# Convolution pairs and decay matrices handed out between attention units, and a different set of buffers at the start

## The chip, the cores and the metric

The kernel runs on one core of a Trainium2 chip. The metric is the time of one execution on the device in microseconds. The engines are named as in the profile: PE (matrix products, with PEld for its weight loads), DVE (vector), ACT (activations), POOL (GpSimd), and SP, whose queue issues nearly all DMA transfers.

## The reference

Four transformer layers on one sequence of 256 tokens of width 1024, all in float32: two layers of a first block (latent attention beside a gated linear recurrence, then a feed-forward part), then two layers of a second block. The change is in the mixing of the second block and in the first microseconds of the kernel. The second block's mixing, cut to what matters:

```python
proj = h @ w_in                                   # h = rmsnorm(x)
q, k, v, z, xbc, dt = split(proj)
attn = dilated_attention(rotary(q), rotary(k), v) # 8 heads of 64, softmax under a mask
xbc = silu(causal_depthwise_conv(xbc, conv_w, conv_b))      # 1536 channels, 4 taps
xs, bm, cm = split(xbc)                           # 1024, 256, 256 channels
dt = softplus(dt + dt_bias)
a_cs = cumsum(dt * -exp(a_log))                   # per head, in chunks of 128 tokens
m_mat = (cm . bm) * exp(where(t >= s, a_cs[t] - a_cs[s], -inf))
y = m_mat @ (xs * dt) + carry_over_of_chunk_0 + d_skip * xs
y = grouped_rmsnorm(y * silu(z))
x = x + concat(attn, y) @ w_out
x = x + swiglu(rmsnorm(x))
```

The first layer of the first block begins with `h = rmsnorm(x)` and the projections of `h` to the latents `c_q` (384 columns) and `c_kv` with `k_pe` (288 columns).

## The kernel before

Activations are kept transposed (128 channels on the partitions, 256 tokens along the row). Each weight is streamed from device memory in tiles of up to 128x1024 by `Stream.load`: a DMA into one of three buffers `wf`, a copy rounded to fp32r on ACT (`wh`, line 399), and the remainder by a subtraction on DVE (`wl`, line 400; on POOL for the weight units named in `WL_POOL`). There are six buffers each of `wh` and `wl`. A product of full precision is then three passes on PE (lines 428 to 430: high by high, high by low, low by high), in the two-pass form of lines 449 and 450 in the feed-forward parts.

A scheduler orders the instructions of each engine. It follows the order of the program text where it can and moves instructions forward when, by its own estimate, their inputs and buffers are ready. So the text's order, the number of buffers and the estimates together decide what stands behind what; at run time each engine works through its own list in order.

`layer_b` computes the second block's mixing. Behind the projections come the softplus of `dt` (lines 1038 to 1048, a chain of small DVE instructions), its product with `-exp(a_log)` (`aa`, line 1053), the cumulative sum as a product on PE (lines 1055 and 1056) and, from it, eight decay matrices: `acs` is transposed (line 1068), written to device memory (`ad`, line 1073), read back spread over all partitions (tile `r`, line 1079), and POOL subtracts the column's own value (line 1080) and adds a causal mask (line 1081); ACT takes the exponential (line 1082). Then `attention` runs six units (one group of heads each). A unit is: scores on PE (line 578), mask and maximum on DVE (lines 582, 584), exponentials on ACT (line 588), the division on DVE (line 590), transposes on PE (line 602), a copy on ACT (line 604), and the product with the values on PE (line 613). In the text the six convolution pairs stand behind the attention: a pair is a weight unit of 48 products on PE, the scaling by the norm on DVE (line 1127), one tap on ACT (line 1132) and three on DVE (line 1134) for each of two channel groups, and a gate by tanh (lines 1137 and 1138). The scheduler already lifts these pairs in between the attention units. Behind them come the products of the decay matrices (line 1174) with the chunk products, `d_skip` (line 1154, on POOL), the gate by `z`, the norm and the output projection.

At the start, `norm_prep` splits `x` in two parts (lines 473 and 474) and calls `norm_scale`, which squares and adds mostly on POOL (lines 502 to 506). `WARM` products on a matrix of ones (line 424) stand ahead of the first real products.

## Time and profile before

| | us |
|---|---|
| median of 3 runs | 1481.76 |
| lowest, highest | 1475.6, 1490.52 |
| the profiled execution's own time | 1484.13 |
| span of the profile (first to last instruction) | 1482.3 |
| PE busy | 1441.9 |
| DVE busy | 1146.6 |
| ACT busy | 822.2 |
| POOL busy | 302.5 |

The profiled execution took 1484.13, of which 1482.3 lie between its first and last instruction. All times in the rows below are microseconds from the start of that span. The second block's mixing lies at about 780 to 925 (its layer 0) and 1125 to 1270 (its layer 1). PEclk is the clock granted to PE as a share of its full speed; 0.5 is the lower of its two levels, 1.2 instead of 2.4 GHz.

### The profile page before, as it was taken

How to read it: one execution, taken by the hardware profiler on the slowest of the kernel's cores; microseconds unless marked ns; L12 is line 12 of the kernel's file. 1: busy time of each engine (PE TensorE's matmuls, PEld its weight loads, DVE VectorE, ACT ScalarE, POOL GpSimd, SP SyncE). 2: the span in 40 equal slices, each digit the busy share in tenths (PEclk: the TensorE clock that was granted, in tenths of full speed). 3: DMA queues.
4: the chain of work that ended last, by engine and by line, in shares of the span. 5: the costliest groups of instructions: out<-in, count | busy, mean ns of one | idle time of the engine just before them, and what ended most of it. 6: DMA issues, size and time to landing. Idle time of an engine off the chain costs nothing.

```text
span 1482.3 us, 26346 instructions
## 1 busy us (share of the span) xinstructions
PE 1441.9 (97%) x10176; PEld 1305.3 (88%) x10176; DVE 1146.6 (77%) x1747; ACT 822.2 (55%) x1415; POOL 302.5 (20%) x302
## 2 busy tenths in 40 slices
PE   8999999999999999999999899999999889999998
PEld 7989998888998999888888799888888789988887
DVE  6796788876677867987666999887766799988754
ACT  6665447655474644666445464476545465466643
POOL 3600020000143101100013724500002634510001
PEclk9999999999999999999999899999999789999999
DMA  6633546555654255655555444555556533556553
GB/s 202 216 128 116 174 162 205 193 165 179 195 186 156 92 160 167 199 194 187 157 185 193 123 152 147 165 190 187 155 188 203 154 115 115 171 188 197 167 178 110
DMA packets 85949, 248.77 MB, mean 168 GB/s; under 512 B 8960, under 2 KB 28224, under 8 KB 85824
## 3 DMA queue, kind: packets, MB, share of 16 engines
q1 hardware_dynamic: 85536, 246.56, 52.4%
q8 instruction: 80, 1.31, 0.4%
q10 hardware_dynamic: 288, 0.52, 0.1%
q14 instruction: 45, 0.37, 0.1%
HBM read 245.94 MB, written 1.11 MB: 167 GB/s over the span
## 4 chain that ended last, share of the span: by engine, by line
PE 76%; DVE 11%; DMA 6%; ACT 2%; issue 2%; POOL 1%; SPq 0%; DVEq 0%; POOLq 0%; ACTq 0%
PE mm L449 25%; PE mm L450 13%; PE mm L429 7%; PE mm L430 7%; PE mm L428 7%; PE at L449 7%; DVE wl L400 4%; PE at L450 4%; DMA wf<-in_wa 3%; DMA wf<-in_wb 2%; DVE t L1134 2%; ACT wh L399 2%; PE at L578 1%; DVE xs L474 1%; PE rc L872 1%
## 5 line engine op out<-in xcount | busy, mean ns | idle before, releaser
L400 DVE TENSOR_TENSOR wl<-wf,wh 128x1024 fp32r<-128x1024 f32 (+2 forms) x500 | 578.8, 1167 | 178.9 <-ACT wh L399 175.9
L399 ACT ACTIVATE wh<-wf 128x1024 fp32r<-128x1024 f32 (+3 forms) x508 | 491.4, 970 | 341.9 <-PE mm L429 90.6
L449 PE MATMUL mm<-xs,wh 128*128 128x512 f32 x960 | 337.1, 394 | 1.7 <-DVE xs L474 1.6
L450 PE MATMUL mm<-xs,wl 128*128 128x256 f32 x960 | 268.7, 281 | 0.0
L449 PEld LDWEIGHTS mm<-xs,wh 128*128 128x128 f32 x960 | 179.7, 187 | 42.7 <-DVE xs L474 1.4
L428 PE MATMUL mm<-xs,wh 128*128 128x256 f32 x704 | 208.2, 296 | 0.3 <-ACT q L750 0.3
L430 PE MATMUL mm<-xs,wl 128*128 128x256 f32 x704 | 206.6, 293 | 0.7 <-DVE wl L400 0.7
L429 PE MATMUL mm<-xs,wh 128*128 128x256 f32 x704 | 207.2, 294 | 0.0
L502 POOL TENSOR_TENSOR m<-x 128x512 f32<-128x512 f32 x27 | 35.7, 1322 | 769.8 <-DVE x L655 616.9
L450 PEld LDWEIGHTS mm<-xs,wl 128*128 128x128 f32 x960 | 181.7, 189 | 0.5
L449 PE MATMUL at<-xs,wh 128*128 128x512 f32 x448 | 157.8, 394 | 0.1
L430 PEld LDWEIGHTS mm<-xs,wl 128*128 128x128 f32 x704 | 139.5, 198 | 3.8 <-issue 2.6
L428 PEld LDWEIGHTS mm<-xs,wh 128*128 128x128 f32 x704 | 139.4, 198 | 3.9 <-issue 2.5
L429 PEld LDWEIGHTS mm<-xs,wh 128*128 128x128 f32 x704 | 139.6, 198 | 2.7 <-issue 2.3
L450 PE MATMUL at<-xs,wl 128*128 128x256 f32 x448 | 126.1, 281 | 0.0
L429 PE MATMUL mm<-r,wh 128*128 128x256 f32 x384 | 109.2, 285 | 0.0
L430 PE MATMUL mm<-r,wl 128*128 128x256 f32 x384 | 108.6, 284 | 0.0
L428 PE MATMUL mm<-r,wh 128*128 128x256 f32 x384 | 107.9, 284 | 0.5 <-DVE x L559 0.5
L449 PEld LDWEIGHTS at<-xs,wh 128*128 128x128 f32 x448 | 83.9, 187 | 19.3 <-PE mm L450 0.4
L449 PE MATMUL mm<-t,wh 128*128 128x512 f32 x256 | 90.7, 395 | 0.0
L449 PE MATMUL mm<-h,wh 128*128 128x512 f32 x256 | 90.7, 395 | 0.0
L450 PEld LDWEIGHTS at<-xs,wl 128*128 128x128 f32 x448 | 84.8, 189 | 0.1
(331 smaller groups left out, 2817.7 us busy)
## 6 DMA issues: line engine op xcount, KB each, us to landing
wf<-in_fa SPq DMA_DIRECT2D x120, 512.0 KB, 3.9
wf<-in_fb SPq DMA_DIRECT2D x120, 512.0 KB, 4.1
wf<-in_wa SPq DMA_DIRECT2D x100, 512.0 KB, 4.3
wf<-in_wb SPq DMA_DIRECT2D x72, 512.0 KB, 3.7
wf<-in_fa SPq DMA_DIRECT2D x32, 192.0 KB, 2.4
...
```

Of the source, the lines that this page charges most:

```text
L399: S.activation(wh[:, :c], f, AF.Copy)
L400: (G if self.i in self.pool else V).tensor_tensor(out=wl[:, :c], in0=f, in1=wh[:, :c].bitcast(F32), op=ALU.subtract)
L428: PE.matmul(ps, lhsT=sh, rhs=mh, start=start, stop=False)
L429: PE.matmul(ps, lhsT=sh, rhs=ml, start=False, stop=False)
L430: PE.matmul(ps, lhsT=sl, rhs=mh, start=False, stop=stop)
L449: PE.matmul(wide, lhsT=wh[:, j, c0:c0 + P], rhs=xs[k], start=k == 0, stop=False)
L450: PE.matmul(wide[:, 1], lhsT=wl[:, j, c0:c0 + P], rhs=xs[k][:, 0], start=False, stop=k == tot - 1)
L474: V.scalar_tensor_tensor(out=dstl, in0=src, scalar=scale, in1=dsth.bitcast(F32), op0=ALU.mult, op1=ALU.subtract)
L502: G.tensor_tensor(out=z, in0=x[:, c:c + 2], in1=x[:, c:c + 2], op=ALU.mult)
L578: PE.matmul(ps[:, h], lhsT=q, rhs=k[:, 0:n * P], start=True, stop=True)
L872: PE.matmul(ps[o:o + ms, g], lhsT=zb[:, 0:ms], rhs=zb.rearrange("p (n a h) -> p n a h", a=2, h=h)[:, :, 1], start=True, stop=True, tile_po ...
L1134: V.scalar_tensor_tensor(out=cv[:, m], in0=xp[:, m, j:j + T], scalar=w(j), in1=cv[:, m], op0=ALU.mult, op1=ALU.add)
```

## The change

Four things are changed together.

In `layer_b` the convolution pairs become a function `conv_pair`, and so does the making of a decay matrix. The first pair is computed ahead of the softplus; `attention` calls `between(u)` in each of its six units, which gives out one more pair (units 0 to 4), the loads of all eight matrices (unit 0) and one matrix's arithmetic (units 1 to 5); the remaining three follow behind.

The matrix's arithmetic is now ACT's: for each of four heads a Relu of `acs - row` (with scale -1 and the column's value as bias), then one exponential with scale -1. The causal mask is not added any more; instead two of the three chunk products (`cb`) are multiplied by the triangle `triu` on DVE, where ACT only copied them. `d_skip` leaves POOL: it is folded into the addition of the chunk's result, one DVE instruction for each of two channel groups instead of one for both. `WL_POOL` is empty, so that all weight remainders are DVE's.

In the first layer the latent projections are given out ahead of the norm's scale, whose squares are now made on ACT and added on DVE.

The first four weight tiles are loaded into the four buffers `h` (not in use that early) instead of `wf`, and `WARM` goes from 9 to 14.

```diff
     WFB, WSB = 3, 6
-    WARM = 9
-    WL_POOL = (7, 9)
+    WARM = 14
+    EARLY = 4
+    WL_POOL = ()
...
             self.pool = WL_POOL if name.startswith("wb") else ()
+            self.early = EARLY if name == "wa0" else 0
...
-                wf = wp.tile([P, 1024], F32, tag="wf", name=nm("wf"), bufs=WFB)
+                if self.early:
+                    self.early -= 1
+                    wf = sb("h", [P, 1024])
+                else:
+                    wf = wp.tile([P, 1024], F32, tag="wf", name=nm("wf"), bufs=WFB)
...
-    def norm_scale(eps):
-
+    def norm_scale(eps, pool=True):
+
+        if not pool:
+            acc = sb("m", [P, 2, T])
+            sq = sb("m", [P, 2, T])
+            for c in (0, 2, 4, 6):
+                z = sq if c else acc
+                S.activation(z, x[:, c:c + 2], AF.Square)
+                if c:
+                    V.tensor_tensor(out=acc, in0=acc, in1=sq, op=ALU.add)
+            a = acc[:, 0]
+            V.tensor_tensor(out=a, in0=a, in1=acc[:, 1], op=ALU.add)
+            return rsqrt(token_sums(a), 2, 1.0 / D, eps)
...
-    def norm_prep(gname, eps):
+    def norm_prep(gname, eps, between=None):
+
         xs = cp.tile([P, NC, 2, T], F32R, tag="xs", name=nm("xs"))
-        xh, xl = xs[:, :, 0], xs[:, :, 1]
         for c in range(NC):
-            split(xh[:, c], xl[:, c], x[:, c], fm(gname, c))
-        r = norm_scale(eps)
-        rb = bcast_rows(r, "rc")
-        return [xh[:, c] for c in range(NC)], [xl[:, c] for c in range(NC)], [xs[:, c] for c in range(NC)], r, rb
+            split(xs[:, c, 0], xs[:, c, 1], x[:, c], fm(gname, c))
+        xh, xl = [xs[:, c, 0] for c in range(NC)], [xs[:, c, 1] for c in range(NC)]
+        if between:
+            between(xh, xl)
+        r = norm_scale(eps, between is None)
+        return xh, xl, [xs[:, c] for c in range(NC)], r, bcast_rows(r, "rc")
...
+                if between:
+                    between(u)
                 pt = psq(next(tags)).rearrange("p (h k) -> p h k", k=P)
...
+        def latents(xh, xl):
+            for n in (384, 288):
+                lat.append([psm(), psm()])
+                lin_tm([p[:, :n] for p in lat[-1]], st.next() + st.next(), xh, xl, n)
+
+        xh, xl, _, r, rb = norm_prep(f"nmix_a{l}", EPS1, latents if l == 0 else None)
         if l == 1:
+            latents(xh, xl)
...
+        conv = {}
+        pairs = [4, 5, 0, 1, 2, 3]
+        c4 = []
+
+        def conv_pair():
+            i = len(conv)
+            p = pairs[i]
+            if i % 2 == 0:
+                c4.append(sb("t", [P, 2, 2, T]))
+            ps = psm().rearrange("p (m t) -> p m t", m=2)
+            u = st.next()
+            for m in range(2):
+                lin_fm(ps[:, m], u, m * P, xh, xl)
+            xp = sb("Z", [P, 2, T + 4])
+            G.memset(xp[:, :, 0:3], 0.0)
+            V.tensor_tensor(out=xp[:, :, 3:T + 3], in0=ps, in1=rows(rb, 2), op=ALU.mult)
+            cv = c4[-1][:, i % 2]
+            for m in range(2):
+                c = 2 * p + m
+                w = lambda j: wh2[:, 4 * c + j:4 * c + j + 1]
+                S.activation(cv[:, m], xp[:, m, 0:T], AF.Identity, scale=w(0), bias=wh2[:, 48 + c:49 + c])
+                for j in range(1, 4):
+                    V.scalar_tensor_tensor(out=cv[:, m], in0=xp[:, m, j:j + T], scalar=w(j), in1=cv[:, m],
+                                           op0=ALU.mult, op1=ALU.add)
+            tz = sb("m", [P, 2, T])
+            S.activation(tz, cv, AF.Tanh)
+            V.scalar_tensor_tensor(out=cv, in0=tz, scalar=1.0, in1=cv, op0=ALU.add, op1=ALU.mult)
+            conv[p] = cv
+
+        conv_pair()
...
-        pT = psq("rc")
-        PE.transpose(pT[0:32, 0:P], acs.rearrange("p t h -> p (t h)"), ident)
-        arow = sb("hv", [32, 2, P])
-        S.activation(arow[:, 0], pT[0:32, 0:P], AF.Copy)
-        S.activation(arow[:, 1], pT[0:32, 0:P], AF.Exp)
-        ad = dp.tile([32, 2, P], F32, tag="ad", name=nm("ad"), bufs=1)
-        nc.sync.dma_start(out=ad, in_=arow)
+
         decay = {}
-        neg4 = neg.rearrange("p (o t) -> p o t", o=1).to_broadcast([P, 4, P])
-        for g, t, q4 in itertools.product(range(2), repeat=3):
-            h0 = 8 * g + 4 * q4
-            E = sb("r", [P, 4, P])
-            nc.sync.dma_start(out=E, in_=ad[16 * t + h0:16 * t + h0 + 4, 0].partition_broadcast(P))
-            G.tensor_tensor(out=E, in0=E, in1=bc(acs[:, t], h0, 4, P), op=ALU.subtract)
-            G.tensor_tensor(out=E, in0=E, in1=neg4, op=ALU.add)
-            S.activation(E, E, AF.Exp)
-            decay[g, t, q4] = E
+        loaded = []
+
+        def decay_rows():
+            pT = psq("rc")
+            PE.transpose(pT[0:32, 0:P], acs.rearrange("p t h -> p (t h)"), ident)
+            arow = sb("hv", [32, 2, P])
+            S.activation(arow[:, 0], pT[0:32, 0:P], AF.Copy)
+            S.activation(arow[:, 1], pT[0:32, 0:P], AF.Exp)
+            ad = dp.tile([32, 2, P], F32, tag="ad", name=nm("ad"), bufs=1)
+            nc.sync.dma_start(out=ad, in_=arow)
+            for g, t, q4 in itertools.product(range(2), repeat=3):
+                h0 = 8 * g + 4 * q4
+                E = sb("r", [P, 4, P])
+                nc.sync.dma_start(out=E, in_=ad[16 * t + h0:16 * t + h0 + 4, 0].partition_broadcast(P))
+                decay[g, t, q4] = E
+                loaded.append((E, t, h0))
+            for j in range(2):
+                nc.sync.dma_start(out=into[64 * j:64 * j + 64], in_=ad[16 + j:32:2, 1].partition_broadcast(64))
+
+        def decay_exp():
+            E, t, h0 = loaded.pop(0)
+            for h in range(4):
+                S.activation(E[:, h], E[:, h], AF.Relu, scale=-1.0, bias=acs[:, t, h0 + h:h0 + h + 1])
+            S.activation(E, E, AF.Exp, scale=-1.0)
+
         into = sb("h", [P, 8, P])
-        for j in range(2):
-            nc.sync.dma_start(out=into[64 * j:64 * j + 64], in_=ad[16 + j:32:2, 1].partition_broadcast(64))
-
-
-        qT = sb("t", [P, 4, T])
-        kT = sb("OF", [P, T])
-        ps = psq("at")
-        for t in range(2):
-            PE.transpose(ps[:, t * P:t * P + P], ak[t], ident)
-        S.activation(kT, ps[:, 0:T], AF.Copy)
-        for t in range(2):
-            ps = psq("at").rearrange("p (c k) -> p c k", c=4)
-            for c in range(4):
-                PE.transpose(ps[:, c], aq[t][:, c * P:c * P + P], ident)
-            S.activation(qT[:, :, t * P:t * P + P], ps, AF.Copy, scale=0.125)
+
+        def between(u):
+            if u == 0:
+                decay_rows()
+            else:
+                decay_exp()
+            if u < 5:
+                conv_pair()
...
-        mh, ml = attention(groups, qk, lambda a, i: av[a][:, i % 2], (dil0, dil1), *oT, ("at", "rc"), AH_B)
+        mh, ml = attention(groups, qk, lambda a, i: av[a][:, i % 2], (dil0, dil1), *oT, ("at", "rc"), AH_B, between)
+
+        while loaded:
+            decay_exp()
...
-        for p in range(4):
-            o = fmc[f"dsk{l}"][0] + 2 * p
-            G.tensor_tensor(out=conv[p], in0=conv[p], in1=bc(pfm, o, 2, T), op=ALU.mult)
...
-            S.activation(cb.rearrange("p g t -> p (g t)"), ps[:, 0:T], AF.Copy)
+            if i < 2:
+                V.tensor_tensor(out=cb, in0=ps[:, 0:T].rearrange("p (g t) -> p g t", g=2),
+                                in1=triu.rearrange("p (o t) -> p o t", o=1).to_broadcast([P, 2, P]), op=ALU.mult)
+            else:
+                S.activation(cb.rearrange("p g t -> p (g t)"), ps[:, 0:T], AF.Copy)
...
-            V.tensor_tensor(out=conv[p], in0=conv[p], in1=py, op=ALU.add)
+            for m in range(2):
+                V.scalar_tensor_tensor(out=conv[p][:, m], in0=conv[p][:, m], scalar=fm(f"dsk{l}", 2 * p + m), in1=py[:, m],
+                                       op0=ALU.mult, op1=ALU.add)
```

In the order of the instructions this shows at three places. The first is POOL in layer 0's second block, from the last step of the queries' rotation on (`r` are the decay matrices, `Z` the convolution's input). Before:

```order
L1014 TENSOR_TENSOR q_9019<-q_9019,rt_1528_9027 128x8x16
L400 TENSOR_TENSOR wl_9524<-wf_9522,wh_9523 128x1024
L400 TENSOR_TENSOR wl_9530<-wf_9528,wh_9529 128x1024
L1126 MEMSET Z_9507 128x2x3
L1080 TENSOR_TENSOR r_9072<-r_9072,acs_9060 128x512
L1080 TENSOR_TENSOR r_9077<-r_9077,acs_9060 128x512
L1081 TENSOR_TENSOR r_9072<-r_9072,msk 128x512
L1080 TENSOR_TENSOR r_9082<-r_9082,acs_9060 128x512
L1081 TENSOR_TENSOR r_9077<-r_9077,msk 128x512
```

Now:

```order
L1039 TENSOR_TENSOR q_9022<-q_9022,rt_1528_9030 128x8x16
L1078 MEMSET Z_9385 128x2x3
L1078 MEMSET Z_9497 128x2x3
L1078 MEMSET Z_9597 128x2x3
L1078 MEMSET Z_9707 128x2x3
```

Twenty large instructions (four remainders, eight subtractions, eight masks) are gone from this place, and only small fills are left until the state products.

The second is ACT at the first attention units of the same layer (`hv` is the transposed cumulative sum, `pr` the probabilities, `Z` and `t` the convolution's input and result, `PT` the transposed probabilities). Before:

```order
L1071 ACTIVATE hv_9067<-rc_9065 32x128
L588 ACTIVATE pr_9143,den_9144<-at_9135,mx_9141 128x128 x4
L588 ACTIVATE pr_9159,den_9160<-rc_9151,mx_9157 128x128 x4
L1137 ACTIVATE m_9367<-t_9294 128x512
L399 ACTIVATE wh_9599<-wf_9598 128x1024
L399 ACTIVATE wh_9605<-wf_9604 128x1024
L1132 ACTIVATE t_9294<-Z_9431,wh_1596_9292 128x256 x2
L604 ACTIVATE PT_9172<-at_9167 128x512
```

Now, from the second softmax to the first transposed probabilities:

```order
L606 ACTIVATE pr_9191,den_9192<-rc_9183,mx_9189 128x128 x4
L1163 ACTIVATE r_9206<-r_9206,acs_9159 128x128 x4
L1163 ACTIVATE r_9208<-r_9208,acs_9159 128x128 x4
L1163 ACTIVATE r_9210<-r_9210,acs_9159 128x128 x4
L404 ACTIVATE wh_9648<-wf_9647 128x1024
L1163 ACTIVATE r_9212<-r_9212,acs_9159 128x128 x4
L1164 ACTIVATE r_9206<-r_9206 128x512
L404 ACTIVATE wh_9654<-wf_9653 128x1024
L1163 ACTIVATE r_9214<-r_9214,acs_9159 128x128 x2
L1164 ACTIVATE r_9208<-r_9208 128x512
L1084 ACTIVATE t_9323<-Z_9385,wh_1529_9035 128x256 x2
L1163 ACTIVATE r_9214<-r_9214,acs_9159 128x128
```

The Relus of four matrices and part of a fifth, which need loads to have landed, now stand on ACT between the second softmax and the copy of the first transposed probabilities.

The third is ACT in the opening (`xs` is the split input, `m` the squares, `wh` a weight's high part). Before:

```order
L473 ACTIVATE xs_154<-x,pfm 128x256 x2
L399 ACTIVATE wh_90<-wf_89 128x768
L473 ACTIVATE xs_154<-x,pfm 128x256 x2
L399 ACTIVATE wh_97<-wf_96 128x768
L473 ACTIVATE xs_154<-x,pfm 128x256 x2
```

Now:

```order
L478 ACTIVATE xs_159<-x,pfm 128x256 x2
L508 ACTIVATE m_276<-x 128x512
L404 ACTIVATE wh_90<-h_89 128x768
L478 ACTIVATE xs_159<-x,pfm 128x256 x2
L508 ACTIVATE m_277<-x 128x512
L404 ACTIVATE wh_97<-h_96 128x768
L478 ACTIVATE xs_159<-x,pfm 128x256 x2
```

A square of 128x512 now stands ahead of each of the first three weight copies, and the copies read from `h`.

## Rows read from the trace of the kernel before

**Rows 1.** The page's first part: PE's busy time, share of the span, instructions.

```profile
PE 1441.9 (97%) x10176; PEld 1305.3 (88%) x10176; DVE 1146.6 (77%) x1747; ACT 822.2 (55%) x1415; POOL 302.5 (20%) x302
```

**Rows 2.** Waits of PE: who waited for whom, us in total, times, longest.

```profile
PE rc L602 <- DVE pr L590: 12.8, 4, 5.4
PE rc L1055 <- DVE aa L1053: 5.2, 2, 3.0
```

**Rows 3.** Busy time in stretches: PE, PEld, DVE, ACT, POOL; PEclk, DMA share, GB/s.

```profile
804.60:820.00 15.40, 13.11 (x61) 11.62 (x61) 9.02 (x17) 6.84 (x26) 5.73 (x5) 0.67 0.54 156
832.70:847.00 14.30, 8.90 (x42) 7.13 (x42) 14.30 (x13) 4.25 (x11) 13.96 (x10) 0.64 0.17 55
...
855.00:860.00 5.00, 5.00 (x42) 4.31 (x42) 5.00 (x10) 3.53 (x6) 0.00 (x0) 1.00 0.71 240
...
1151.50:1168.00 16.50, 13.52 (x58) 12.22 (x58) 8.84 (x18) 6.67 (x26) 4.83 (x3) 0.59 0.43 136
1181.70:1192.00 10.30, 7.27 (x31) 6.08 (x31) 10.30 (x10) 2.81 (x7) 10.30 (x9) 0.67 0.18 57
1196.40:1205.00 8.60, 4.59 (x20) 3.61 (x20) 8.60 (x17) 6.29 (x14) 0.38 (x2) 0.80 0.16 61
```

**Rows 4.** DVE's timeline: start, length, instruction, count, idle before.

```profile
804.72 2.27 DVE L1048 SCALAR_TENSOR_TENSOR dtt<-dtt,pol 128x32 f32<-128x32 f32 x1
...
830.23 2.70 DVE L1134 SCALAR_TENSOR_TENSOR t<-Z,wh,t 128x256 f32<-128x256 f32 x2
...
849.27 0.47 DVE L1134 SCALAR_TENSOR_TENSOR t<-Z,wh,t 128x256 f32<-128x256 f32 x1
...
851.05 0.68 DVE L590 TENSOR_TENSOR pr<-pr,den 128x512 f32<-128x512 f32 x1
...
1154.05 0.19 DVE L1048 SCALAR_TENSOR_TENSOR dtt<-dtt,pol 128x32 f32<-128x32 f32 x1
```

**Rows 5.** DVE's groups from 800 to 925: busy us, mean ns, idle before.

```profile
L400 DVE TENSOR_TENSOR wl<-wf,wh 128x1024 fp32r<-128x1024 f32 x24 | 32.0, 1336 | 1.1 <-ACT wh L399 1.1
L1134 DVE SCALAR_TENSOR_TENSOR t<-Z,wh,t 128x256 f32<-128x256 f32 x36 | 25.4, 738 | 0.3 <-ACT t L1132 0.3
L590 DVE TENSOR_TENSOR pr<-pr,den 128x512 f32<-128x512 f32 x6 | 7.7, 1277 | 0.0
L1138 DVE SCALAR_TENSOR_TENSOR t<-m,t 128x512 f32<-128x512 f32 x6 | 6.7, 1110 | 0.9 <-ACT m L1137 0.8
```

**Rows 6.** POOL's groups over the whole span, both layers: busy us, mean ns, idle before.

```profile
L1081 POOL TENSOR_TENSOR r<-r,msk 128x512 f32<-128x512 f32 x16 | 24.0, 1510 | 0.0
L1080 POOL TENSOR_TENSOR r<-r,acs 128x512 f32<-128x512 f32 x16 | 22.5, 1424 | 3.8 <-DMA r<-ad 3.8
L400 POOL TENSOR_TENSOR wl<-wf,wh 128x1024 fp32r<-128x1024 f32 x8 | 19.9, 2492 | 7.8 <-ACT wh L399 7.8
```

**Rows 7.** ACT's timeline at the first softmax of layer 0's second block.

```profile
813.16 0.37 ACT L588 ACTIVATE pr<-at,mx 128x128 f32<-128x128 f32 x1
813.42 0.19 ACT L588 ACTIVATION_READ_ACCUMULATOR pr<-at,mx 128x1 f32 x1
```

**Rows 8.** The 16 loads of line 1079 (`r<-ad`): us from issue to landing.

```profile
DMA to landing us min/median/max: 4.3/5.9/8.2
```

**Rows 9.** The opening: timelines of PE and ACT.

```profile
10.15 0.69 PE L429 MATMUL mm<-wl,xs 128*128 128x384 f32 x1 [2.14 <-DVE wl L400]
...
13.20 0.52 PE L430 MATMUL mm<-wh,xs 128*128 128x384 f32 x1
...
15.53 0.34 PE L430 MATMUL mm<-wh,xs 128*128 128x384 f32 x1
...
29.90 0.39 PE L430 MATMUL mm<-xs,wl 128*128 128x256 f32 x1 [0.74 <-DVE wl L400]
...
13.24 0.85 ACT L399 ACTIVATE wh<-wf 128x768 fp32r<-128x768 f32 x1 [1.96 <-DMA wf<-in_wa]
...
27.53 1.06 ACT L399 ACTIVATE wh<-wf 128x1024 fp32r<-128x1024 f32 x1 [2.87 <-DMA wf<-in_wa]
```

60 lines of the change are left out of this document (22 added, 38 removed).

## The prediction

> **What bounds the kernel now.** First the busy shares [rows 1]: PE is busy 1441.9 of 1482.3 us, 97%. PE sets the time, and whatever the change does can only come out of the 40 us in which PE is idle and out of products that run at the lower clock. So next I looked for where these lie: the stretches with their granted clock, and PE's list of waits. In the second block's mixing PE waits for DVE at two kinds of place [rows 2]: 12.8 us in four waits for the divided probabilities (line 590) ahead of the transposes, and 5.2 us in two waits for `aa`, the end of the softplus chain, ahead of the cumulative sum.
>
> Five stretches hold these waits [rows 3]. Idle time is length less PE's busy time: 2.3 and 5.4 us in layer 0; 3.0, 3.0 and 4.0 in layer 1: 17.7 together. In each of the five the clock also falls to its lower level once PE has waited; length times (1 - PEclk) is 15.4 x 0.33 = 5.1, 14.3 x 0.36 = 5.1, 16.5 x 0.41 = 6.8, 10.3 x 0.33 = 3.4, 8.6 x 0.20 = 1.7, together 22.1. Some half clock falls into the idle time itself; I take off 1.5 as an estimate. What PE loses there is then about 17 us in layer 0 and 21 in layer 1, 38 in all. That is the purse of the main part of the change.
>
> Why is DVE late? It is itself full there (14.30 of 14.30, 10.30 of 10.30 [rows 3]), but many of its instructions take far longer than they need to. Two conv taps take 2.70 us at 830, while one takes 0.47 at 849 [rows 4]. The last softplus step, a 128x32 instruction, takes 2.27 us at 804.7 and 0.19 in the other layer [rows 4]. POOL is busy 13.96 of 14.30 us in the slow stretch and not at all at 855 to 860 [rows 3]: DVE's instructions stretch when POOL runs large ones.
>
> **The change part by part.** *POOL's work leaves.* Per layer, eight subtractions of 1.42, eight masks of 1.51 and four remainders of 2.49 us go [rows 6], besides four `d_skip` products. What this frees on DVE I sum from layer 0's groups [rows 5], each against its undisturbed length [rows 4]: taps 25.4 - 36 x 0.47 = 8.5; divisions 7.7 - 6 x 0.68 = 3.6; gates, of the same shape, 6.7 - 6 x 0.68 = 2.6; the softplus step 2.27 - 0.19 = 2.1. That is 16.8 us per layer.
>
> *DVE's added work.* Four remainders come over: 4 x 1.34 = 5.3 at the disturbed mean [rows 5], an upper bound. Two triangle products of 128x256 at no more than 0.47 each, and `d_skip` as eight half-width instructions instead of four full ones, 8 x 0.47 - 4 x 0.68: another 2. DVE's balance is 16.8 - 7.3 = 9.5 us less work per layer. It can also take back time in which it waits for PE at half clock: it is idle 6.4 us in the first stretch of layer 0 and 7.7 in that of layer 1 [rows 3]. So on DVE's path the gain is 9.5 at least and 16 to 17 at most per layer; on PE's path it is 17 and 21.
>
> *The cumulative sum.* In the order DVE's chain up to `aa` is unchanged, four remainders among it; without POOL's remainder beside it, its last step ends 2.1 us sooner in layer 0, where PE waits 2.2. Most of that wait goes, and with it the reason for the half clock behind it.
>
> *ACT's added work.* 32 Relus of 128x128 per layer. No row shows a Relu with a bias; the nearest is the softmax's exponential of the same size and bias, 0.37 long, with the next instruction starting 0.26 after it [rows 7]. Bounds are 8.3 and 11.8 us per layer; I take 0.30 each, 9.6, since neighbours overlap. The exponentials stay. ACT is busy 4.25 of 14.30 us in the slow stretch [rows 3], so the sum fits; what matters is order. The Relus of four matrices and more stand ahead of the first `PT` copy. Following the lists from the second softmax: four times 1.2 us of Relus, two weight copies of 1.06 [rows 9], two exponentials, the fifth matrix's first three Relus, two taps and a tanh, about 11 us, until that copy. PE in this time has the products of one and a half pairs and a full pair, some 100 at 0.12 us (42 in 5.00 [rows 3]), 12 us, before it needs `PT`. That leaves a margin of one or two microseconds: ACT's new work is hidden, barely.
>
> The Trainium skill, "ScalarE: Activation LUTs", section "What ACT_TABLE_LOAD costs", gives an activation with a bias pointer as some 280 ns and 0.833 ns per element, of which about 93 ns overlap with the next one. By that a Relu would be an estimated 0.29 us and the 32 of a layer 9.4, in place of 9.6; no run here shows it yet.
>
> *The loads of the matrices.* They are issued from SP at the same place as before, behind one more weight load. Landing takes 4.3 to 8.2 us [rows 8]; POOL used to stand waiting for the first, now ACT does, with weight copies, taps and `PT` queued behind it, and PE behind those. The order puts two softmaxes and three more instructions between the store and the first Relu, so I cost this at nothing; if the landing takes its maximum instead of its median 5.9, the margin above is gone and PE waits about 2 us.
>
> *What is late next.* With the taps short, I expect PE to wait for about 1 us at the cumulative sum, 1 at the later transposes, 1 to 2 for a remainder that now queues on DVE, and 2 at the output projection, whose inputs still pass over POOL (the gate by `z`) and DVE. That is 5 to 6 us per layer, in waits shorter than those of [rows 3], all of over 2 us, behind which the clock fell. So of 17 I count 12 in layer 0, of 21 I count 15 in layer 1; both lie between DVE's bounds.
>
> *The opening.* PE starts its second kind of product at 10.15 after a wait of 2.14 for the first remainder, runs at half clock (a product 0.52 long at 13.2, 0.34 at 15.5), and later the first weight behind the constants keeps ACT waiting 2.87 until 27.53 and PE until 29.90 [rows 9]. With POOL's squares gone the first remainder should come about 1.5 us sooner, although ACT now makes a square ahead of it (about 0.55, half of the copy of 1024 columns at 27.53 [rows 9]); the longer warm-up leaves no gap. With four loads in buffers of their own, the wait of 1.96 for the fourth at 13.24 goes too [rows 9]. What ends the stage is the load that ACT waits for at 27.53; its buffer comes free behind these copies, so by an estimate of 1.5 to 3.5 us earlier, and the load with it. Gain 3; bounds 0 (the load comes no earlier) and 4.5 (all of it counts). Behind 30 us PE is full, so it is kept.
>
> The sum is 12 + 15 + 3 = 30 us off the profiled execution's 1484.1, which is 1454. That execution lies 2.4 above the median of 1481.8, so against the median I forecast **1452**.
>
> **The rivals.** *Everything recovered*: PE never waits for long; 38 + 4.5 - 2 = 40.5 us, 1441. For it: DVE's bound of 16 to 17 nearly reaches layer 0's 17. Against it: DVE stays full.
>
> *One fall of the clock per layer stays*, because one of the late waits passes 2 us. Price: the first stretch of layer 0 shows it, 5.1 of clock; two layers, 10 us: 1462. The Trainium skill, "TensorE: Matmul & The Clock Gate", section "HAM oscillation — how this bites in real kernels", describes waits each of which makes the stretch behind it start at the lower clock again; this trace agrees in all five stretches [rows 3].
>
> *ACT becomes the late engine* (slower): the first Relu waits for its load in ACT's list, taps and `PT` come late, and through the two `Z` buffers and four PSUM banks every pair stalls PE. This decides the sign if PE then loses more per layer than now, over 19 us, which is about three waits of 2.3 with their 5 us of clock each, 22 per layer: 44 against 38, less the opening's 3: 1485. For it: the thin margin. Against it: ACT was idle for 10 of 14.3 us, and a load that lands in 6.
>
> *The change does not do what it says*: the scheduler had lifted the pairs already, so handing them out may be no change, and the time would come from POOL's relief alone. That gives DVE's lower bound, 9.5 per layer, and an opening of 0: 1463.
>
> **How the numbers follow.** Chances: forecast 0.50 (1445 to 1459), everything recovered 0.12 (1438 to 1445), one fall or POOL's relief alone together 0.27 (1459 to 1471), ACT late 0.11 (1471 to 1500). The range of 1440 to 1470 leaves out most of the last case and little else. One per cent is 14.8 us, about the spread of the three runs shown and about what a measurement of this kernel can tell from no change. Faster than 1467: 0.50 + 0.12 + most of 0.27, 0.82. Slower than 1496.6: a third of the last case, 0.04. The rest, 0.14, is no change.
>
> **What would show it.** In the profile after: no waits of PE of over 2 us for line 608 (the division) or for `aa`; PEclk at full in both mixings; taps at 0.4 to 0.5 each; POOL nearly idle until the state products; ACT busier by 9 to 10 us per layer; the first remainder at about 8.5 and pair products from about 26. Wrong would be: a wait of ACT for `r<-ad` over 2 us, PE waiting for ACT's `PT` or for remainders, or stretches of half clock without a wait ahead of them.

## The result, and the profile after

The changed kernel takes 1457.05 us (median of four, 1454.24 to 1460.24) against 1481.55 for the kernel before: a ratio of 0.9836, 95% interval 0.9802 to 0.9871. That is 24.5 us or 1.6% faster. The forecast was 1452, with a range of 1440 to 1470. The profiled execution took 1456.76 us, 27.4 less than that of before.

The first part of the page after (busy time, share of the span, instructions) answers to [rows 1]:

```profile
PE 1425.7 (98%) x10186; PEld 1290.3 (89%) x10186; DVE 1117.2 (77%) x1769; ACT 839.2 (58%) x1477; POOL 221.6 (15%) x248
```

PE is idle for 29 us in place of 40. Its waits after (who waited for whom, us in total, times, longest) answer to [rows 2]. Line 608 is the division, which was line 590; 1131 is the cumulative sum, which was 1055:

```profile
PE mm L433 <- DVE m L575: 3.6, 2, 2.3
PE rc L1131 <- DVE aa L1129: 3.1, 2, 1.8
PE mm L433 <- ACT wh L404: 2.8, 2, 1.7
...
PE mm L435 <- DVE wl L405: 2.3, 3, 0.8
PE rc L622 <- DVE pr L608: 1.5, 2, 0.8
```

The waits for the divided probabilities have gone from 12.8 us to 1.5, those for `aa` from 5.2 to 3.1. What is last now is `m` at the output projection (line 575). Six stretches of both mixings, read as [rows 3] (length, busy time of PE, PEld, DVE, ACT, POOL, then PEclk):

```profile
800.00:804.00 4.00, 2.25 (x20) 2.04 (x20) 3.86 (x10) 2.33 (x5) 2.00 (x3) 1.00 0.41 123
...
842.00:847.00 5.00, 3.47 (x28) 3.09 (x27) 4.93 (x10) 5.00 (x12) 0.11 (x1) 1.00 0.39 120
1133.00:1138.00 5.00, 3.61 (x31) 3.40 (x31) 4.76 (x13) 2.66 (x5) 2.99 (x5) 1.00 0.54 143
...
1176.00:1181.00 5.00, 3.46 (x27) 3.09 (x27) 4.93 (x10) 5.00 (x12) 0.00 (x0) 1.00 0.36 113
900.00:908.00 8.00, 5.34 (x43) 5.03 (x41) 6.56 (x13) 4.20 (x5) 4.11 (x5) 1.00 0.50 164
908.00:914.00 6.00, 6.00 (x37) 5.95 (x38) 4.94 (x7) 1.45 (x2) 5.15 (x7) 0.72 0.39 128
```

In each of the first four PE still loses 1.4 to 1.8 us, but the granted clock stays at its upper level (PEclk 1.00). Only behind the output projection of layer 0, where PE is idle for 2.7 us, does the clock fall once: 6.0 x 0.28 = 1.7 us. Of the five falls of [rows 3] none is left in its place.

DVE's groups in layer 0, 796 to 910, answer to [rows 5] (busy us, mean ns, idle before):

```profile
L405 DVE TENSOR_TENSOR wl<-wf,wh 128x1024 fp32r<-128x1024 f32 x29 | 36.5, 1259 | 4.8 <-ACT wh L404 4.7
L1086 DVE SCALAR_TENSOR_TENSOR t<-Z,wh,t 128x256 f32<-128x256 f32 x36 | 15.5, 477 | 0.0
L608 DVE TENSOR_TENSOR pr<-pr,den 128x512 f32<-128x512 f32 x6 | 4.1, 688 | 0.1
L1090 DVE SCALAR_TENSOR_TENSOR t<-m,t 128x512 f32<-128x512 f32 x6 | 4.1, 688 | 0.7 <-ACT m L1089 0.7
```

Taps went from 738 ns to 477, divisions from 1277 to 688, gates from 1110 to 688. ACT's group of Relus in the same stretch:

```profile
L1163 ACT ACTIVATE r<-r,acs 128x128 f32<-128x128 f32 x32 | 10.2, 395 | 2.0 <-DMA r<-ad 2.0
```

They overlap, and 10.2 us is the time in which at least one of them runs. What one costs shows where several stand in a row:

```profile
832.82 2.16 ACT L1163 ACTIVATE r<-r,acs 128x128 f32<-128x128 f32 x7
```

Less the length of the last, 2.16 - 0.40 us hold six of them, 0.29 from one start to the next, so 32 take 9.4 us. ACT waits 2.0 us for the first matrix. PE and ACT in the opening (start, length, idle before) answer to [rows 9]:

```profile
8.02 0.44 PE L434 MATMUL mm<-wl,xs 128*128 128x384 f32 x1 [0.37 <-DVE wl L405]
...
25.88 0.39 PE L433 MATMUL mm<-xs,wh 128*128 128x256 f32 x1 [1.68 <-ACT wh L404]
...
24.77 1.06 ACT L404 ACTIVATE wh<-wf 128x1024 fp32r<-128x1024 f32 x1 [3.31 <-DMA wf<-in_wa]
```

To see where the time went I cut the run into stages, by DVE's last addition to the residual in each: line 675 ends a feed-forward, line 577 a second-block mixing. In the kernel after these additions start at:

```profile
778.32 0.41 DVE L675 TENSOR_TENSOR x<-x,mm 128x256 f32<-128x256 f32 x1
...
927.42 0.41 DVE L577 TENSOR_TENSOR x<-x,m 128x256 f32<-128x256 f32 x1
...
1112.74 0.41 DVE L675 TENSOR_TENSOR x<-x,mm 128x256 f32<-128x256 f32 x1
...
1260.79 0.41 DVE L577 TENSOR_TENSOR x<-x,m 128x256 f32<-128x256 f32 x1
...
1445.04 0.88 DVE L675 TENSOR_TENSOR x<-x,mm 128x256 f32<-128x256 f32 x2 [4.53 <-PE mm L455]
```

In the kernel before (lines 655 and 559) the same five start at:

```profile
781.79 0.41 DVE L655 TENSOR_TENSOR x<-x,mm 128x256 f32<-128x256 f32 x1
...
945.66 0.41 DVE L559 TENSOR_TENSOR x<-x,m 128x256 f32<-128x256 f32 x1
...
1128.82 0.41 DVE L655 TENSOR_TENSOR x<-x,mm 128x256 f32<-128x256 f32 x1
...
1291.89 0.41 DVE L559 TENSOR_TENSOR x<-x,m 128x256 f32<-128x256 f32 x1
...
1472.73 0.87 DVE L655 TENSOR_TENSOR x<-x,mm 128x256 f32<-128x256 f32 x2 [4.39 <-PE mm L450]
```

So up to the first of these mixings 3.5 us are won, in the mixings 163.9 - 149.1 = 14.8 and 163.1 - 148.0 = 15.1, and in the two feed-forwards behind them, which nobody touched, 2.2 and 3.4 us are lost. The last two figures were in no step of the prediction. The cut is good to about 1 us: in layer 0 DVE's last addition starts 5.8 us behind PE's first product of the feed-forward in the kernel before and 4.6 in the kernel after. Cut by the first and last products of the feed-forwards on PE, the mixings win 13.6 and 15.5 and the feed-forwards lose 1.0 and 3.9.

### The profile page after: what moved, and what is told of

The parts are those of the page before. It is cut to its first block, busy times and chain, and to the rows that moved or that the text cites. A ratio compares the mean times of both kernels' runs of the same rounds, so it can differ in the third digit from the quotient of the medians.

```text
span 1455.0 us, 26376 instructions
## 1 busy us (share of the span) xinstructions
PE 1425.7 (98%) x10186; PEld 1290.3 (89%) x10186; DVE 1117.2 (77%) x1769; ACT 839.2 (58%) x1477; POOL 221.6 (15%) x248
## 4 chain that ended last, share of the span: by engine, by line
PE 87%; DVE 6%; ACT 2%; DMA 2%; issue 2%; POOL 1%; SPq 0%; POOLq 0%; DVEq 0%; ACTq 0%
PE mm L454 25%; PE mm L455 13%; PE mm L434 11%; PE mm L435 11%; PE mm L433 11%; PE at L454 7%; PE at L455 4%; DVE wl L405 2%; DVE xs L479 1%; PE at L596 1%; DMA wf<-in_wb 1%; ACT wh L404 1%; PE at L633 1%; PE rc L897 1%; PE at L622 1%
## 5 line engine op out<-in xcount | busy, mean ns | idle before, releaser
L405 DVE TENSOR_TENSOR wl<-wf,wh 128x1024 fp32r<-128x1024 f32 (+3 forms) x504 | 577.2, 1155 | 182.0 <-ACT wh L404 179.9
L454 PEld LDWEIGHTS mm<-xs,wh 128*128 128x128 f32 x960 | 179.7, 187 | 43.9 <-DVE xs L479 2.9
L433 PE MATMUL mm<-xs,wh 128*128 128x256 f32 x704 | 203.2, 289 | 1.7 <-ACT wh L404 1.7
L434 PE MATMUL mm<-xs,wh 128*128 128x256 f32 x704 | 202.7, 288 | 0.0
L455 PEld LDWEIGHTS mm<-xs,wl 128*128 128x128 f32 x960 | 181.4, 189 | 0.6
L454 PE MATMUL at<-xs,wh 128*128 128x512 f32 x448 | 158.5, 395 | 0.6 <-DVE pr L663 0.6
L518 POOL TENSOR_TENSOR m<-x 128x512 f32<-128x512 f32 x24 | 31.9, 1330 | 770.7 <-DVE x L675 621.3
L435 PEld LDWEIGHTS mm<-xs,wl 128*128 128x128 f32 x704 | 135.4, 192 | 5.3 <-DVE wl L405 3.3
L433 PEld LDWEIGHTS mm<-xs,wh 128*128 128x128 f32 x704 | 135.4, 192 | 3.4 <-ACT wh L404 1.9
L434 PEld LDWEIGHTS mm<-xs,wh 128*128 128x128 f32 x704 | 135.5, 193 | 1.6 <-issue 1.2
```

The costliest lines, as they stand in the source:

```text
L405: (G if self.i in self.pool else V).tensor_tensor(out=wl[:, :c], in0=f, in1=wh[:, :c].bitcast(F32), op=ALU.subtract)
L433: PE.matmul(ps, lhsT=sh, rhs=mh, start=start, stop=False)
L434: PE.matmul(ps, lhsT=sh, rhs=ml, start=False, stop=False)
L435: PE.matmul(ps, lhsT=sl, rhs=mh, start=False, stop=stop)
L454: PE.matmul(wide, lhsT=wh[:, j, c0:c0 + P], rhs=xs[k], start=k == 0, stop=False)
L455: PE.matmul(wide[:, 1], lhsT=wl[:, j, c0:c0 + P], rhs=xs[k][:, 0], start=False, stop=k == tot - 1)
```

## The experiments

The theory of the prediction: DVE was late because POOL's large instructions held its instructions up, and taking them away gives the gain; the order of the work is of second rank. The first rival: it is the order, pairs and matrices between the units, that counts. The second: ACT's new work only just fits. Twelve runs were made in three groups, beside which the kernel before had medians of 1486.23, 1485.12 and 1487.31 us; so between groups ratios are compared, not times. The mixings are cut as above, each from the one profiled execution of its run. That execution was the slowest of four where POOL is relieved without pieces (1479.94 us) and with the matrices alone (1473.5), and the fastest of ten with the pairs alone (1471.44).

| kernel | median us | ratio to before, 95% | mixing 0 | mixing 1 |
|---|---|---|---|---|
| before | 1481.55 | 1 | 163.9 | 163.1 |
| after | 1457.05 | 0.9836 (0.9802 to 0.9871) | 149.1 | 148.0 |
| after again | 1455.49 | 0.9789 (0.9755 to 0.9824) | 149.2 | 147.8 |
| old opening | 1461.11 | 0.9816 (0.9791 to 0.984) | 151.0 | 150.0 |
| opening alone | 1482.76 | 0.998 (0.9956 to 1.0005) | 164.3 | 164.4 |
| pieces, POOL's work kept | 1483.2 | 0.9979 (0.9958 to 0.9999) | 160.9 | 163.9 |
| POOL relieved, no pieces | 1473.72 | 0.9911 (0.9883 to 0.9939) | 158.8 | 160.4 |
| relieved, pairs alone in pieces | 1477.8 | 0.9953 (0.9929 to 0.9977) | 155.6 | 162.7 |
| relieved, matrices alone in pieces | 1471.17 | 0.9892 (0.9857 to 0.9928) | 158.3 | 159.1 |
| idle work on POOL | 1476.89 | 0.9934 (0.9914 to 0.9954) | 161.6 | 160.4 |
| remainders back on POOL | 1471.83 | 0.9905 (0.9873 to 0.9936) | 158.5 | 157.7 |
| Relus twice | 1461.0 | 0.9826 (0.9794 to 0.9858) | 153.4 | 149.9 |
| three small steps | 1460.72 | 0.983 (0.98 to 0.9859) | 151.7 | 153.3 |
| masks and copy | 1448.45 | 0.9739 (0.9713 to 0.9766) | 147.5 | 149.7 |

### The opening, taken away and alone

The old opening in the changed kernel:

```diff
-    WARM = 14
-    EARLY = 4
+    WARM = 9
+    EARLY = 0
...
-        xh, xl, _, r, rb = norm_prep(f"nmix_a{l}", EPS1, latents if l == 0 else None)
+        xh, xl, _, r, rb = norm_prep(f"nmix_a{l}", EPS1)
...
+        latents(xh, xl)
         pcq, pkv = lat
```

> The changed kernel with the old opening: loads through three buffers, squares on POOL, nine warm-up products. Between the two traces the same weight copies run 3.5 us earlier from 130 us on, so theory one (the opening gives what it shows there, and it is kept) expects 1457 + 3.5 = about 1460.5 us, with the first copy of 1024 columns back at 27.5 us instead of 24.8. The rival (the opening is worth nothing, because what is won is lost again to the wait and the half clock at 24 to 31 us) expects 1457. The trace decides better than the time: the products of a feed-forward came at two paces (391 and 399 ns for one of 512 columns), which moves the total by up to 4 us either way, and I shall take the copies' starts at 130 to 200 us.

The other way round, the kernel before with the hunks of the opening alone (also the squares on ACT and the buffers of tag `h`):

```diff
-    WARM = 9
+    WARM = 14
+    EARLY = 4
...
-        xh, xl, _, r, rb = norm_prep(f"nmix_a{l}", EPS1)
+        xh, xl, _, r, rb = norm_prep(f"nmix_a{l}", EPS1, latents if l == 0 else None)
```

> The kernel before with the new opening alone. Theory one expects 1481.5 - 3.5 = about 1478 us, copies 3.5 us earlier from 130 us on, and the second-block mixings as before: about 20 and 22 us lost by PE. The rival expects 1481.5.

The first copy of 1024 columns comes at 27.2 us with the old opening and at 25.3 with the new one in the kernel before; 27.5 and 24.8 in the two kernels themselves. In the seven other kernels with this opening unchanged and in the repeat of the changed one it lies between 24.4 and 25.8. So the opening brings about 2.5 us there, as theory one says. The mark named beforehand was the weight copies from 130 to 200 us. They come 3.5 us later than in the changed kernel with the old opening and 4.1 earlier than in the kernel before with the new opening alone, but the mark does not decide: in the other kernels with the new opening they lie anywhere from 1.8 us ahead of the changed kernel to 3.0 behind it. Up to the first second-block mixing the gain stays true only on average: those kernels reach it at 775.9 to 781.6 us, the two with the old opening at 780.3 and 781.8, because the first block in between has waits and falls of the clock that come and go. In the time of the whole it can't be told from nothing: the opening alone has an interval that reaches 1, and the kernel without it lies between the two measurements of the kernel with it.

### Two halves: POOL's relief and the pieces

The pieces, but POOL's work back:

```diff
-            for h in range(4):
-                S.activation(E[:, h], E[:, h], AF.Relu, scale=-1.0, bias=acs[:, t, h0 + h:h0 + h + 1])
-            S.activation(E, E, AF.Exp, scale=-1.0)
+            G.tensor_tensor(out=E, in0=E, in1=bc(acs[:, t], h0, 4, P), op=ALU.subtract)
+            G.tensor_tensor(out=E, in0=E, in1=neg.rearrange("p (o t) -> p o t", o=1).to_broadcast([P, 4, P]), op=ALU.add)
+            S.activation(E, E, AF.Exp)
...
-    WL_POOL = ()
+    WL_POOL = (7, 9)
```

(and `d_skip` and the mask of the chunk products as in the kernel before).

> The changed kernel with POOL's work back (subtraction and mask of each matrix, d_skip products, two weight units' remainders on POOL), but pairs and matrices still handed out between the attention's units. Theory one (contention of POOL with DVE) expects taps back at about 0.7 us, PE's loss in each mixing back above 15 us, and 1472 to 1478 us. The rival (the order counts) expects 1457 to 1463 us with taps as in the changed kernel.

DVE's taps in layer 0, 797 to 925, and PE's waits over the whole run:

```profile
L1087 DVE SCALAR_TENSOR_TENSOR t<-Z,wh,t 128x256 f32<-128x256 f32 x36 | 24.8, 718 | 0.7 <-ACT t L1085 0.7
```

```profile
PE rc L623 <- DVE pr L609: 14.6, 2, 8.2
PE rc L1132 <- DVE aa L1130: 10.9, 2, 5.9
```

Theory one holds by its marks: taps are long again and both waits are back, longer than before. The time, 1483.2, is above the ranges of both theories. The order alone gives 2 us of 30 in the mixings. What each part of POOL's work is worth, this run does not tell; the remainders alone follow below.

POOL relieved, but nothing handed out:

```diff
-        def between(u):
-            if u == 0:
-                decay_rows()
-            else:
-                decay_exp()
-            if u < 5:
-                conv_pair()
+        decay_rows()
+        while loaded:
+            decay_exp()
...
-        mh, ml = attention(groups, qk, lambda a, i: av[a][:, i % 2], (dil0, dil1), *oT, ("at", "rc"), AH_B, between)
-        while loaded:
-            decay_exp()
+        mh, ml = attention(groups, qk, lambda a, i: av[a][:, i % 2], (dil0, dil1), *oT, ("at", "rc"), AH_B)
+        for _ in range(6):
+            conv_pair()
```

(The first pair's call ahead of the softplus goes too, and the transposes of queries and keys are back behind the matrices.)

> The changed kernel with the pairs and the decay matrices back at their old places in the program (all matrices ahead of the attention, all pairs behind it); the decay still on ACT, remainders on DVE, the mask and d_skip folded in. Theory one (POOL's large instructions stretch DVE's, and that was the loss) expects nearly all of the gain: taps at 0.48 us, PE's loss in the two mixings 8 to 12 us in all more than the changed kernel's 14 at most, a time of 1457 to 1465. The rival (the order is what counts; ACT's Relus of eight matrices ahead of the softmaxes stand in their way) expects ACT late ahead of the attention, waits of PE of over 2 us for the divided probabilities and a time of 1470 to 1480.

DVE's taps in layer 0, 797 to 925, and two of PE's waits over the whole run:

```profile
L1086 DVE SCALAR_TENSOR_TENSOR t<-Z,wh,t 128x256 f32<-128x256 f32 x36 | 15.9, 473 | 0.0
```

```profile
PE mm L433 <- ACT wh L404: 5.7, 6, 1.8
PE mm L433 <- DVE m L575: 4.6, 2, 2.3
```

Here theory one fails. DVE's instructions are as short as in the changed kernel, and still the mixings win only 5.1 and 2.7 us. The long waits for the divided probabilities are gone; PE waits for weight copies of ACT, remainders and the output projection instead, 0.5 to 2.5 us each. Of the rival's marks the time is seen, and so is ACT being late (2.9 of the 5.7 us for its weight copies lie in the mixings, and 2.5 us for `PT`), but no wait for the divided probabilities is over 2 us. The sizes are those of the slowest of four executions, 6.2 us above their median; it reaches the first mixing 3.3 us later than the changed kernel, so a part of that lies ahead of the mixings. By the medians this kernel wins 12.5 us in all, with what the opening gives, where the changed kernel wins 24.5 and 31.8.

So the two edits need each other, and I asked which of the pieces it is. Pairs alone handed out, all matrices ahead; then matrices alone handed out, all pairs behind:

```diff
+        decay_rows()
+        while loaded:
+            decay_exp()
         def between(u):
-            if u == 0:
-                decay_rows()
-            else:
-                decay_exp()
             if u < 5:
                 conv_pair()
```

> The changed kernel with the eight decay matrices ahead of the attention as before, on ACT, and the pairs alone handed out. The kernel with POOL relieved but nothing handed out kept only 9 of the 24 us. Theory P (it is the pairs that have to stand between the units, so that PE has products while DVE divides) expects 1457 to 1462 us. Theory A (it is ACT's 42 Relus and exponentials ahead of the softmaxes that made that kernel slow) expects 1470 us or more, with PE waiting for ACT ahead of the attention's products.

```diff
         def between(u):
             if u == 0:
                 decay_rows()
             else:
                 decay_exp()
-            if u < 5:
-                conv_pair()
...
+        for _ in range(6):
+            conv_pair()
```

(Here too the first pair's call ahead of the softplus goes.)

> The changed kernel with the six pairs behind the attention as before and the matrices alone handed out. Theory P expects about what the kernel with nothing handed out gave, 1470 to 1475 us. Theory A expects 1457 to 1462 us.

Both theories fall: neither half of the pieces shows a gain by itself. Their ratios of 0.9953 and 0.9892 have intervals that overlap that of the kernel with nothing handed out (0.9911). The two mixings take 318.3 and 317.4 us together, against 319.2 with nothing handed out and 297.1 with both. The waits only change their place, to the inputs of the output projection. PE's waits over the whole run with the pairs alone, and with the matrices alone:

```profile
PE mm L434 <- DVE r L479: 7.6, 5, 3.4
PE mm L433 <- ACT wh L404: 5.1, 3, 1.9
```

```profile
PE mm L434 <- DVE r L479: 4.9, 2, 3.8
PE mm L435 <- DVE wl L405: 3.9, 3, 1.6
```

`r` from line 479 is the split of the gated output, the last DVE work ahead of the output projection. My reading is that ACT and DVE have to get rid of both kinds of work beneath the attention, and that whichever kind stays outside comes back as a queue at the end of the mixing; no run shows that queue by itself.

### Contention by itself

Eighteen products a layer on POOL, which nobody reads or waits for, three behind each pair:

```diff
+            for _ in range(3):
+                G.tensor_tensor(out=noise, in0=cv.rearrange("p m t -> p (m t)"), in1=msk, op=ALU.mult)
             conv[p] = cv
```

> The changed kernel with idle work on POOL: three products of 128x512 behind each convolution pair, 18 in a layer, into a tile that nobody reads. Theory one (POOL's large instructions stretch DVE's beside them, whatever they are for) expects taps of 0.6 to 0.75 us in place of 0.48, PE's loss in the mixings up again by 5 to 10 us a layer, and 1467 to 1477 us. The rival (DVE was slowed, and PE kept waiting, because their work waited for POOL's results) expects taps of 0.48 us and 1457 us, since nothing waits for these products.

The products and DVE's taps beside them, 797 to 925:

```profile
L1093 POOL TENSOR_TENSOR noise<-t,msk 128x512 f32<-128x512 f32 x18 | 28.6, 1588 | 14.5 <-DVE t L1091 13.6
```

```profile
L1087 DVE SCALAR_TENSOR_TENSOR t<-Z,wh,t 128x256 f32<-128x256 f32 x36 | 22.9, 681 | 0.0
...
L1080 DVE TENSOR_TENSOR Z<-mm,rb 128x512 f32<-128x512 f32 x6 | 4.1, 681 | 0.0
```

Theory one holds. Work for nothing on POOL makes the taps 0.68 us long and takes back 24.9 of the 29.9 us that the mixings had won. The 0.68 is a mean: 27 of the 36 taps have no such product beside them and keep 0.45 to 0.48 us, and eight of the other nine last 1.1 to 1.5. `Z`, whose one input lies in PSUM, keeps its length of 0.68, also in the two of six that ran beside a product.

Two weight units' remainders back to POOL, with all else as in the changed kernel:

```diff
-    WL_POOL = ()
+    WL_POOL = (7, 9)
```

> The changed kernel with the remainders of two weight units given back to POOL, four instructions of about 2.5 us a layer. The contention theory: POOL's idle products cost 20 us for 36 of about 1.4 us, 0.4 us of time per us of POOL's work; four remainders of 2.5 us in two layers are 20 us of POOL, so 8 us, less 8 remainders of 1.26 us that DVE no longer makes where they count: 1457 to 1465 us. The rival (DVE's load alone decides, so every instruction off DVE helps) expects 1449 to 1455.

It costs 19.1 us in the mixings, more than either theory allowed, for eight instructions. DVE's and POOL's timelines at the end of the softplus chain of layer 0, and PE's behind it, show why:

```profile
801.64 4.64 POOL L405 TENSOR_TENSOR wl<-wf,wh 128x1024 fp32r<-128x1024 f32 x2
801.76 2.27 DVE L1124 SCALAR_TENSOR_TENSOR dtt<-dtt,pol 128x32 f32<-128x32 f32 x1
804.06 2.33 DVE L1129 SCALAR_TENSOR_TENSOR aa<-dtt,an 128x16 f32<-128x16 f32 x2
...
806.54 0.61 PE L1131 MATMUL rc<-aa,cst 128*128 128x32 f32 x2 [6.88 <-DVE aa L1129]
```

POOL's two remainders end at 803.96 (half of 4.64 on) and 806.28. DVE's step of 128x32, 0.19 us long when alone [rows 4], starts 0.12 behind the first and ends 0.07 after it, at 804.03; `aa` starts behind the second and ends 0.11 after it, at 806.39. So DVE's instruction isn't slowed in proportion, it stands still until POOL's has ended, and PE stands for 6.88 us, where it stood for 1.75 in the changed kernel. What POOL costs is not its length but who is caught behind it. The Trainium skill, "SBUF — State Buffer", section "Who interferes with whom", states this as a lock: a DVE instruction with two SBUF inputs and a POOL instruction that reads SBUF exclude each other, the one that issues first keeps the port for its whole length, and a DVE instruction with one SBUF input and not in a two-port mode isn't touched. The traces agree: the two instructions here with the first two points, `Z` above with the last.

### ACT's margin

```diff
+            for h in range(4):
+                S.activation(E[:, h], E[:, h], AF.Relu)
             S.activation(E, E, AF.Exp, scale=-1.0)
```

> The changed kernel with each Relu followed by a second one on the same data, 32 more of 128x128 a layer on ACT, which change no value. If ACT's margin was as thin as predicted (1 to 2 us ahead of the first PT copy), about 8 of the 10 us a layer come through: 1470 to 1477 us, with PE waiting for PT or for weight copies of ACT. The rival (ACT has room everywhere between the units, since it was idle for 10 of 14 us) expects 1457 to 1461.

ACT's two groups of Relus, 797 to 925:

```profile
L1163 ACT ACTIVATE r<-r,acs 128x128 f32<-128x128 f32 x32 | 10.6, 405 | 1.3 <-DMA r<-ad 1.3
L1165 ACT ACTIVATE r<-r 128x128 f32<-128x128 f32 x32 | 8.2, 316 | 0.0
```

Seven of the second kind in a row:

```profile
824.58 1.49 ACT L1165 ACTIVATE r<-r 128x128 f32<-128x128 f32 x7
```

One takes 0.20 us from start to start, so ACT has 6.4 us more a layer, not the 10 expected. They cost 4.3 in one mixing and 1.9 in the other. No wait of PE for `PT` appears, but the other mark of the first theory does: in each mixing PE waits once for a weight copy of ACT, 1.0 and 1.4 us, where the changed kernel has no such wait. PE's waits in layer 0's mixing are hardly longer in all, 6.6 us for 6.0; what is lost is clock, 0.74 of it granted from 842 to 862 us and 0.83 from 1182 to 1202, where the changed kernel had 1.00. By the time, 1461.0 at the edge of its range, the rival is the nearer one: ACT's room is wider than the 1 to 2 us predicted, but the added work does not go unnoticed.

### The changed kernel once more

> The changed kernel once more, unchanged. Two things are asked. The ratio to the kernel before on another chip job: 0.9836 again if it holds. And the pace of the second block's feed-forward products: if the pace of 391 or 399 ns belongs to the program, both feed-forwards of the second block come at 399 ns again; if it is settled anew in each execution (behind the last wait of PE ahead of the stage), at least one may come at 391, which alone moves the time by 3 to 4 us.

The same program had a profiled execution of 1450.86 us, 5.9 shorter than the first one. The mixings agree within 0.3 us; 5.4 of the 5.9 lie in the two feed-forwards behind them, 183.2 and 181.0 us against 185.3 and 184.2. The same products in the last feed-forward, 1316 to 1371, in the first profile of this program and in the second (mean ns behind the busy time):

```profile
L454 PE MATMUL mm<-xs,wh 128*128 128x512 f32 x109 | 38.7, 399 | 0.0
```

```profile
L454 PE MATMUL mm<-xs,wh 128*128 128x512 f32 x99 | 34.5, 391 | 0.0
```

So the pace belongs to the execution, not to the program: the second answer expected.

### A better version

Three small edits at places where PE waits: the masks loaded behind the first four wide weight loads, the first step of each inverse root on DVE instead of POOL, and the copy of the first block's `Z` (line 879; 5.64 us on POOL in layer 1) on ACT.

```diff
-        G.tensor_scalar(out=y, in0=src, scalar1=scale, scalar2=eps, op0=ALU.mult, op1=ALU.add)
+        V.tensor_scalar(out=y, in0=src, scalar1=scale, scalar2=eps, op0=ALU.mult, op1=ALU.add)
...
-                G.tensor_copy(out=Zv[:, :, 0], in_=kv[:, :, 0])
+                S.activation(Zv[:, :, 0], kv[:, :, 0], AF.Copy)
...
-            G.tensor_scalar(out=rg2, in0=rg, scalar1=0.5, scalar2=None, op0=ALU.mult)
+            V.tensor_scalar(out=rg2, in0=rg, scalar1=0.5, scalar2=None, op0=ALU.mult)
```

> The changed kernel with three small edits at places where its trace shows PE waiting: the masks are loaded behind the first four wide weight loads (2.5 us of waiting and 1.7 of half clock at 24 to 31), the first step of each inverse root and the halving of the last one go from POOL to DVE (1.0 to 1.1 us each beside DVE's work, 0.2 alone; PE waits 2.7 us at 904 for what hangs on two of them), and a copy of 128x512 in the first block goes from POOL to ACT (5.64 us in layer 1, PE waits 2.4 and has 1.7 of half clock). If these waits are the last to end at their places: 2 to 4 + 1 to 4 per layer + 4, so 1443 to 1449 us. The rival (another input is late by as much at each place) expects 1455 to 1457.

A miss, 0.983. At 40 us the copies are 1.1 us ahead, and PE's wait for that copy in layer 1 is gone, but in layer 0, where the copy takes only 0.66 us on POOL, ACT is now late by 1.6 us and the clock falls for 1.7; and the inverse roots on DVE stand in DVE's queue, so that PE waits 3.5 us for the rows made from them. That the copy makes ACT late in layer 0 isn't shown: PE waits 2.1 to 2.4 us for the same result of ACT (line 845) in three kernels above that have the copy on POOL. The mixings get 2.6 and 5.3 us longer. So I kept two of the three, the copy in layer 1 alone:

```diff
-        if l == 0:
-            masks()
...
         pair_fm(hf)
+        if l == 0:
+            masks()
...
-                G.tensor_copy(out=Zv[:, :, 0], in_=kv[:, :, 0])
+                if l == 1:
+                    S.activation(Zv[:, :, 0], kv[:, :, 0], AF.Copy)
+                else:
+                    G.tensor_copy(out=Zv[:, :, 0], in_=kv[:, :, 0])
```

> The changed kernel with the two of the three small edits that the trace of their joint run showed to pay: the masks behind the first four wide weight loads (copies 1.1 us earlier at 40 us), and the copy in the first block on ACT in layer 1 alone, where PE's wait of 2.4 and its half clock of 1.7 went; in layer 0, where it cost 1.6 and 1.7, it stays on POOL, and the inverse roots stay there too. If these add up: 1457 - 1 - 3.5 = about 1452.5. The rival (what is won is taken back by the next wait, as in the joint run) expects 1457.

1448.45 us (six executions, 1444.39 to 1450.64), against 1455.49 for the changed kernel in the same group (four, 1450.86 to 1459.88). It beats both kernels: each of its six lies below all eight executions of the changed kernel, though the intervals of the two ratios just overlap. No run takes the two edits apart. The first mixing begins at 773.6 us in place of 778.1, the 4.5 expected. PE's waits in the first block of layer 1, 400 to 560, in the changed kernel's second profile and in this one:

```profile
PE rc L897 <- POOL Z L879: 2.4, 1, 2.4
```

```profile
PE at L622 <- DVE pr L608: 0.6, 1, 0.6
PE at L844 <- ACT t L845: 0.2, 1, 0.2
```

## Why the prediction was right, and where it was not

The time of 1457.05 lies 5 us above the forecast and well inside the range. What POOL does to DVE was right, and the sum of what comes back was right; that the sum fits so well is in part luck. The prediction priced POOL's relief alone at 19 of the 27 us in the mixings and left 8 to the order, where the runs show 8 and 22; and the mixings' 3 us above the forecast made up for part of the 5.6 lost in the feed-forwards. The steps one by one:

- **What bounds the kernel, and the purse.** Right. PE's waits and the half clock behind them were the loss in the mixings, and nearly all that was won came out of them.
- **Layer 0 by 12, layer 1 by 15.** The mixings gave 14.8 and 15.1. Right in layer 1, and 2.8 too low in layer 0 (1.6 if cut by PE).
- **DVE's instructions shorten when POOL leaves.** Right in each number: 0.477 a tap (0.47 said), 0.688 a division and a gate (0.68 said), 1.26 a remainder (1.34 as the upper bound). The idle work on POOL shows the cause.
- **DVE's balance of 9.5 us a layer as the gain's lower bound.** Wrong, and so was the rival built on it, that handing out does nothing and POOL's relief alone gives 1463. With that relief and nothing handed out the mixings win 5.1 and 2.7 us, not 9.5 each. Less work on the engine that PE waits for is no bound from below: as I read it, PE waits for the instruction that stands last in a list, and where the list is in the wrong order the time freed is idle. The prediction held the order for a matter of second rank; the runs show that 22 of the 30 us need it, and need both kinds of pieces.
- **The cumulative sum.** Half right. The wait of 2.2 in layer 0 was to go almost wholly; 1.8 are left there, of 3.1 in both layers. What did go is the half clock behind it. The softplus step did shorten, from 2.27 us to 0.19; what the sum still waits for, no run takes apart.
- **ACT's added work, 9.6 us a layer, barely hidden.** The size is right, 9.4, or 0.29 a Relu from start to start against the 0.30 taken. "Barely" is too strong: 6.4 us more of Relus a layer cost 4.3 and 1.9 us. By the Trainium skill, "ScalarE: Activation LUTs", section "What ACT_TABLE_LOAD costs", the estimate was 0.29; the trace agrees, with 0.29.
- **The loads of the matrices.** Right: ACT waits 2.0 us for the first in layer 0, and no wait of PE answers to it.
- **What is late next.** About right: the sum, the transposes, remainders and the output projection, as listed, none of them over 2.33 us. But one fall of the clock stayed, behind the output projection of layer 0; it is the rival "one fall" at one place of two, and it cost 1.7 us rather than 5. It stood behind a wait of 2.33 us; the same wait of 2.33 in the better version has no fall behind it, so that a wait passes 2 us does not settle it. PE waiting for remainders was named both as expected and as a sign of being wrong: it did, three times, 0.8 us at most.
- **The opening, 3 us.** Right in the trace: 2.8 at the first wide copy, 3.5 at the first mixing, PE's second kind of product at 8.02 and the wide ones at 25.9 where 8.5 and 26 were said. Its price in the first block varies from run to run by more than that. That PE ran there at half clock before isn't what the profile grants: PEclk reads 1.00 from 7 to 14 us, though the products started 0.32 us apart and from 14.6 us on 0.17.
- **What failed by size.** The sum had no term for the feed-forwards: "behind 30 us PE is full, so it is kept" took it that a full PE runs at one pace. In the profiled execution they gave back 2.2 and 3.4 us of the 33 won ahead of them. In the last one that is the pace: a pair of products every 0.353 us where the kernel before had 0.347. In the other it is not, since the kernel before also ran at 0.353 there from 965 us on; 1.2 of the 2.2 us belong to the cut, and the cause of the 1.0 left is open. In the repeat, with 0.347 in both, the same program took 1450.86.

ACT as the late engine did not come. "Everything recovered" did not either: PE still loses 6 to 8 us in each mixing. Two smaller slips of the numbers: 1496.6 to 1500 us is an eighth, not a third, of the last case's 1471 to 1500; and a change of one per cent is well clear of the noise, as four runs gave the ratio to 0.35% either way.
